# A two-layer hybrid transformer trunk on one core: low parts on VectorE, norms in one operation, attention of the first half as one chain

## The chip, the cores and the metric

One core of one Trainium2 chip runs the whole program. The metric is the device time of one execution in microseconds (us), as the median of several runs. Engines are named as in the profile: PE is TensorE (PEld its weight loads), DVE is VectorE, ACT is ScalarE, POOL is GpSimd, SP issues most loads from memory.

## What is computed

1024 tokens of width 1024 go through two layers, each followed by a squared-ReLU MLP (1024 to 4096 and back). Everything is float32.

```python
# layer 0 (even): h = rms_norm(x); one projection h @ w_in gives
#   A: q (4 heads), one shared k and v, index queries (8 heads x 64), index key, index weights
#   B: q, k, v (4 heads) and a forget gate per head
score = sum_j w_idx[j] * relu(q_idx[j] @ k_idx.T)          # causal
idx = top_k(score, 256)                                     # keys kept for each query
oa = softmax(rms_norm(q) @ rms_norm(k)[idx].T * scale) @ v[idx]
ob = softmax(rms_norm(q) @ rms_norm(k).T * scale + c_q - c_k) @ v   # c: cumulative log forget gate
x += concat(oa, ob) @ w_out;  x += relu(rms_norm(x) @ w1)**2 @ w2
# layer 1 (odd): C multi-head latent attention (low-rank q and k/v, rotary part), D Mamba-2 scan
x += concat(oc, y) @ w_out;   x += relu(rms_norm(x) @ w1)**2 @ w2
```

## The kernel before, in words

**Halves and precision.** The 1024 tokens are worked on in two halves of 512. A float32 product is made of three float32r products: each operand is split into a high part (ACT writes it, `whi` for weights, `xnh` for normed activations) and a low part, the rest (`wlo`, `xnl`), and `mm3` issues high x high, high x low and low x high. `split` writes both parts. `piece` loads weights in pieces of 128x1024 (`wraw`, four buffers), splits them into `whi` and `wlo` (three buffers each), and SP issues the loads.

**Who writes the low parts.** `lo_of` is a list that `piece` rotates: up to the first MLP it is five times POOL and once DVE, from there on DVE alone. In `norm_x` POOL writes `xnl` of every second one of eight chunks, DVE that of the others.

**Projections.** `proj_f` gives results with features on partitions, `proj_t` with tokens on partitions; `proj_t` keeps two blocks of 128 tokens in one PSUM bank when its weights are 256 wide, and calls `done` for each. `qk_pair` projects two heads of queries or keys; `head_norms` takes the sum of squares of each head (ACT) and copies the block to `st` (DVE, L656); `rstd_of` makes reciprocal roots on POOL (L279, L280, a power); `normed_T` scales each 128x128 block by its column of `ss` (DVE, L662, eight for a pair), and later turns the blocks on PE (L667).

**What runs beside what.** A Python generator yields after each small step. `beside(gen, rate)` advances one while a projection is written: every `tick` of the projection advances it by `rate` steps. So `rate` sets how densely PE's order mixes attention into projections. `after(n, fn)` puts a step off by n ticks; `finish` writes the rest of a generator at once. Engines then run their lists in order, each waiting on semaphores.

**Selection** (`topk_masks`): 31 rounds find each query's 256th score bit by bit; in each, ACT counts some blocks with a Sign pass (L825), DVE the others (L860), and DVE updates a candidate (L865 to L869). Its end marks ties and writes masks (L888 to L901), one step for each block. The first half's selection has two blocks, the second half's four (three of them counted by ACT).

**Attention.** `pipe` yields three steps a block: weigh an older block (`po`, L551), turn one (transposes L517, copies to `pt` on ACT, L518), score a new one (L540, then `softmax`: exponential on ACT, reciprocal and scaling on DVE, L527 and L528). `fox_blocks` is B, `dsa_blocks` is A. In the first half B runs at rate 1.5 beside projections of both halves, and is finished; A starts after that, at rate 1.7, beside the output projection of B.

Of the kernel before, what the change touches and what calls it, by code (L numbers as in the profile page):

```python
# [36 lines left out]
def trunk(ctx, tc, a, out):  # L37
# [213 lines left out]

    lo_of = [dve]

    def split(hi, lo, src, scale=None, eng=None):

        if scale is None:
            act.activation(hi, src, AF.Copy)  # L257
            (eng or dve).tensor_sub(lo, src, hi.bitcast(F32))  # L258
        else:
            act.activation(hi, src, AF.Copy, scale=scale)  # L260
            dve.scalar_tensor_tensor(lo, src, scale, hi.bitcast(F32), op0=ALU.mult, op1=ALU.subtract)
# [20 lines left out]
    def piece(parts, kc, n, at=0):  # L282


        subs = []
        per = min(kc, 1024 // n)
        for k0 in range(0, kc, per):
            nk = min(per, kc - k0)
            raw, hi, lo = (wp.tile([P, room], dt, name=nm, tag=nm, bufs=bufs)[:, a0:a0 + nk * n]
                           .rearrange("p (k f) -> p k f", k=nk)  # L290
                           for nm, dt, bufs, room, a0 in (("wraw", F32, 4, 1024, 0), ("whi", F32R, 3, 1088, at),
                                                          ("wlo", F32R, 3, 1088, at)))
            c0 = 0
            for ap in parts:
                w = ap.shape[-1]
                nc.sync.dma_start(raw[:, :, c0:c0 + w], ap[k0 * P:(k0 + nk) * P].rearrange("(k p) f -> p k f", p=P))
                c0 += w
            split(hi, lo, raw, eng=lo_of[0])
            lo_of.append(lo_of.pop(0))
            subs.append((k0, nk, hi, lo))  # L300
        return subs
# [13 lines left out]

    def proj_t(xn, subs, n, done):

# [4 lines left out]
        def part(b, sub):  # L322
# [8 lines left out]
            if k0 + nk == kc and b % per == per - 1:  # L331
                for q in range(per):
                    done(b - per + 1 + q, pss[b // per][:, q * n:(q + 1) * n])
# [111 lines left out]
    def norm_x(half, gain, box):  # L445
        flush(box)
        hi, lo = [], []
        for c in range(DC):
            if c % 2 == 0:
                hi.append(xnp.tile([P, 2, HT], F32R, name="xnh", tag="xnh"))  # L450
                lo.append(xnp.tile([P, 2, HT], F32R, name="xnl", tag="xnl"))
            y = tmp(name="xr")
            dve.scalar_tensor_tensor(y, xc(half, c), gain[:, c:c + 1], box["rb"], op0=ALU.mult, op1=ALU.mult)  # L453
            split(hi[-1][:, c % 2], lo[-1][:, c % 2], y, eng=pool if c % 2 else dve)
        return (lambda k: hi[k // 2][:, k % 2]), (lambda k: lo[k // 2][:, k % 2])
# [193 lines left out]

    def head_norms(ps, b, q, ss, heads, width):  # L650

        for h in range(heads):
            junk = tmp((P, 192), name="junk")
            act.activation(junk[:, :width], ps[:, h * width:(h + 1) * width], AF.Square,
                           accum_out=ss[:, b * heads + h: b * heads + h + 1])
        dve.tensor_copy(q, ps[:, :heads * width])  # L656

    def normed_T(st, heads, h, r, dst, gain):

        for b in range(NB):  # L660
            v = st[:, b, h * P:(h + 1) * P]
            dve.tensor_scalar(v, v, r[:, b * heads + h: b * heads + h + 1], None, op0=ALU.mult)  # L662

# [18 lines left out]
    def qk_pair(xn, w_ap, gain, dst):  # L682

        w = piece([w_ap], 8, 256, MOVING)
        st = g([P, NB, 256], name="st")
        ss = small(NB * 2, "ss")
        proj_t(xn, w, 256, lambda b, ps: head_norms(ps, b, st[:, b], ss, 2, P))
        rstd_of(ss, NB * 2, 128.0, "qk")
        for h in range(2):
            normed_T(st, 2, h, ss, dst[h], gain)  # L690

    def even_proj_index(half, xn):
# [17 lines left out]
        def gates(r):  # L710
# [12 lines left out]
            dve.tensor_sub(lf, lf, z)  # L723
            after(3, sums)

# [84 lines left out]
    def topk_masks(accs, Ls, by_act):  # L810
# [77 lines left out]
        for n, L in enumerate(Ls):  # L888
# [14 lines left out]
    def fox_proj(half, xn, pr):  # L903
# [8 lines left out]
        w = piece([w_in[:, EV_VB + pr * 256: EV_VB + (pr + 1) * 256]], 8, 256, MOVING)  # L912
        proj_t(xn, w, 256, lambda b, ps: act.copy(vb[:, b], ps[:, :256]))
        yield
# [50 lines left out]
    def even_dsa_proj(half, xn):  # L965
# [8 lines left out]
        def done(b, ps):  # L974
            head_norms(ps, b, st[:, b], ss, 1, P)
            act.copy(va[:, b * P:(b + 1) * P], ps[:, P:2 * P])

        proj_t(xn, w, 256, done)
        rstd_of(ss, NB, 128.0, "ka")
        normed_T(st, 1, 0, ss, ka, cols["ka"])  # L980
        yield
# [51 lines left out]
    def odd_low_rank(half, xn):  # L1033
# [30 lines left out]
        for name, r, src in (("cq", rq, [(0, 0), (0, 128), (1, 0)]), ("ckv", rkv, [(1, 128), (2, 0)])):  # L1064
            for c, (n, c0) in enumerate(src):
                for b in range(NB):
                    v = st[n][:, b, c0:c0 + P]
                    dve.tensor_scalar(v, v, r[:, b:b + 1], None, op0=ALU.mult)
                h = new_h("low")
# [11 lines left out]
    def mla_proj(half, pr):  # L1081
# [16 lines left out]
        rstd_of(sq, NB * 2, 192.0, "q")  # L1098
        qT, qrT = [[g([P, 2, HT], F32R, name=k) for _ in range(n)] for k, n in (("qT", 2), ("qrT", 1))]
        for h in range(2):  # L1100
            normed_T(qs, 2, h, sq, (qT[h][:, 0], qT[h][:, 1]), qscale[:, 2:3])

# [21 lines left out]
        def done_kv(b, ps):  # L1124
            for h in range(2):
# [13 lines left out]
        dve.tensor_tensor(krs, kr[:, :, None, :].to_broadcast([P, NB, 2, 64]),  # L1139
                          sk3[:, :, :, None].to_broadcast([P, NB, 2, 64]), op=ALU.mult)  # L1140
        for h in range(2):
            normed_T(ks, 2, h, sk, (kT[h][:, 0], kT[h][:, 1]), cols["kcn"])

# [136 lines left out]
    def ssd_scan(half, gi, hs):  # L1280
# [95 lines left out]
        rstd_of(ss, NB, 256.0, "y")  # L1376
        for b in range(NB):
            dve.tensor_scalar(yg[:, b], yg[:, b], ss[:, b:b + 1], None, op0=ALU.mult)
        yield
# [40 lines left out]

    lo_of[:] = [pool] * 5 + [dve]
    box = row_stats(rows)
# [19 lines left out]

    fox = pipe(chain(fox_blocks(0, 0, hs_a), fox_blocks(0, 1, hs_a)), 2)
    dsa = pipe(dsa_a(), 3)
    beside(fox, 1.5)
    run(fox_proj(0, xn, 1))
# [24 lines left out]

# [122 lines left out]
```

## Time and profile before

| what | value |
|---|---|
| median of 3 runs (lowest to highest) | 2816.67 us (2814.97 to 2818.53) |
| profiled execution: time, span | 2815.35 us, 2813.6 us |
| PE busy | 2723.9 us, 97% |
| PE weight loads | 2324.4 us, 83% |
| DVE, ACT, POOL busy | 1738.2, 1256.1, 743.8 us (62%, 45%, 26%) |
| granted clock of PE, mean | 0.988 |
| chain that ended last | PE 75%, DVE 9%, issue 5%, ACT 5%, POOL 3%, DMA 1% |

The first two slices of forty (some 140 us) show PE at 7 and 8 tenths, all later ones 8 or 9 and more. The granted clock is a share of 2.4 GHz; it has two levels, 1.2 GHz and 2.4 GHz, so that 0.83 over a stretch means that a third of it ran at the lower one. Rows of windows give busy time (and number of instructions) of each engine in a stretch; PE's idle time there is the stretch less PE's busy time. A row of a group of instructions gives busy time and mean duration, and after the second bar the engine's idle time just before them with its releasers.

### The profile page before, as it was taken

What the parts mean: (1) busy time and instruction counts of PE and PEld (TensorE: products, weight loads), DVE (VectorE), ACT (ScalarE), POOL (GpSimd) and SP (SyncE); (2) the same over time, 40 slices, a digit from 0 to 9 for tenths busy, and PEclk for the clock granted to TensorE, in tenths of its full rate; (3) what the DMA queues carried; (4) which work ended last, traced back from release to release, by engine and by line L of the source; (5) the groups of instructions that cost most, each with busy time, mean ns of one, the idle gap of its engine ahead of it and who ended that gap; (6) DMA issues with size and microseconds to landing.
All of it is one profiled execution on the core that took longest, in us unless ns stands there. A gap on an engine that the chain in (4) does not pass through costs nothing.

```text
span 2813.6 us, 39104 instructions
## 1 busy us (share of the span) xinstructions
PE 2723.9 (97%) x14509; PEld 2324.4 (83%) x14509; DVE 1738.2 (62%) x3169; ACT 1256.1 (45%) x2446; POOL 743.8 (26%) x878
## 2 busy tenths in 40 slices
PE   7889999999999999999999999999999999999999
PEld 6888877888788898888888889888887788788887
DVE  5775456877864577764567666775466754634434
ACT  4565335599734355543333334554433323332322
POOL 5335433111100212331344410233134430110110
PEclk8999999999999999999999999999999999999999
DMA  6243433334421426853334552685323463333332
GB/s 175 68 139 121 155 111 90 107 103 143 143 75 61 165 84 165 239 182 105 120 105 153 167 178 80 185 248 168 127 98 120 135 217 98 113 98 98 98 97 68
DMA packets 302964, 365.84 MB, mean 130 GB/s; under 512 B 40611, under 2 KB 258606, under 8 KB 302774
## 3 DMA queue, kind: packets, MB, share of 16 engines
q1 hardware_dynamic: 236550, 223.51, 25.8%
q0 software_dynamic: 66224, 139.84, 15.2%
q8 instruction: 114, 1.87, 0.3%
q14 instruction: 76, 0.62, 0.1%
HBM read 292.16 MB, written 68.70 MB: 128 GB/s over the span
## 4 chain that ended last, share of the span: by engine, by line
PE 75%; DVE 9%; issue 5%; ACT 5%; POOL 3%; DMA 1%; POOLq 0%; DVEq 0%; ACTq 0%
PE pm L273 21%; PE pm L274 21%; PE pm L275 21%; PE po L551 3%; PE pa L540 2%; ACT junk L825 1%; PE pa L517 1%; DVE xr L453 1%; DVE wlo L258 1%; PE py L1342 1%; ACT whi L257 1%; DVE st L662 1%; POOL xnl L258 1%; DVE x L468 1%; POOL rsq L493 1%
## 5 line engine op out<-in xcount | busy, mean ns | idle before, releaser
L257 ACT ACTIVATE whi<-wraw 128x1024 fp32r<-128x1024 f32 (+2 forms) x414 | 434.0, 1049 | 604.0 <-PE pm L274 510.3
L258 DVE TENSOR_TENSOR wlo<-wraw,whi 128x1024 fp32r<-128x1024 f32 (+1 forms) x369 | 462.6, 1254 | 207.4 <-ACT whi L257 187.9
L273 PE MATMUL pm<-xnh,whi 128*128 128x512 f32 (+1 forms) x1360 | 547.4, 404 | 6.0 <-ACT xnh L257 4.9
L274 PE MATMUL pm<-xnl,whi 128*128 128x512 f32 (+1 forms) x1360 | 534.2, 393 | 7.8 <-DVE xnl L258 4.6
L275 PE MATMUL pm<-xnh,wlo 128*128 128x512 f32 (+1 forms) x1360 | 534.1, 393 | 0.0
L273 PE MATMUL pm<-h,whi 128*128 128x512 f32 x1024 | 409.5, 401 | 5.2 <-DVE tk L895 4.5
L274 PE MATMUL pm<-h,whi 128*128 128x512 f32 x1024 | 401.8, 392 | 0.7 <-DVE h L258 0.7
L275 PE MATMUL pm<-h,wlo 128*128 128x512 f32 x1024 | 401.9, 392 | 0.0
L468 DVE TENSOR_TENSOR x<-pm,x 128x512 f32<-128x512 f32 x336 | 231.0, 688 | 270.2 <-PE pm L275 265.3
L493 POOL TENSOR_TENSOR rsq<-relu 128x512 f32<-128x512 f32 x128 | 165.9, 1296 | 824.3 <-ACT relu L491 754.9
L274 PEld LDWEIGHTS pm<-xnl,whi 128*128 128x128 f32 (+1 forms) x1360 | 256.5, 189 | 63.9 <-POOL xnl L258 6.9
L273 PEld LDWEIGHTS pm<-xnh,whi 128*128 128x128 f32 (+1 forms) x1360 | 256.6, 189 | 58.3 <-ACT xnh L257 6.4
L275 PEld LDWEIGHTS pm<-xnh,wlo 128*128 128x128 f32 (+1 forms) x1360 | 256.0, 188 | 55.6 <-issue 0.4
L273 PE MATMUL pm<-whi,xnh 128*128 128x256 f32 x1024 | 298.9, 292 | 0.6 <-DVE st L656 0.6
L275 PE MATMUL pm<-whi,xnl 128*128 128x256 f32 x1024 | 288.4, 282 | 2.0 <-POOL xnl L258 1.1
L274 PE MATMUL pm<-wlo,xnh 128*128 128x256 f32 x1024 | 288.4, 282 | 0.0
L273 PEld LDWEIGHTS pm<-h,whi 128*128 128x128 f32 x1024 | 193.4, 189 | 44.1 <-DVE tk L895 5.2
L275 PEld LDWEIGHTS pm<-h,wlo 128*128 128x128 f32 x1024 | 193.0, 188 | 41.3 <-DVE wlo L258 0.2
L274 PEld LDWEIGHTS pm<-h,whi 128*128 128x128 f32 x1024 | 193.4, 189 | 38.8 <-DVE h L258 1.7
L258 DVE TENSOR_TENSOR h<-rsq,h 128x512 fp32r<-128x512 f32 x128 | 95.2, 743 | 181.7 <-ACT h L257 180.3
L273 PEld LDWEIGHTS pm<-whi,xnh 128*128 128x128 f32 x1024 | 196.2, 192 | 3.8 <-DVE st L656 1.0
L275 PEld LDWEIGHTS pm<-whi,xnl 128*128 128x128 f32 x1024 | 196.3, 192 | 2.6 <-POOL xnl L258 1.5
(651 smaller groups left out, 4508.6 us busy)
## 6 DMA issues: line engine op xcount, KB each, us to landing
wraw<-in_mlp_w_dram SPq DMA_DIRECT2D x256, 512.0 KB
wraw<-in_ev_w_in_dram SPq DMA_DIRECT2D x44, 512.0 KB
wraw<-in_od_w_in_dram SPq DMA_DIRECT2D x40, 512.0 KB
wraw<-in_od_w_out_dram SPq DMA_DIRECT2D x24, 512.0 KB
parked<-x POOLq DMA_DIRECT2D x16, 512.0 KB, 4.0
wraw<-in_ev_w_out_dram SPq DMA_DIRECT2D x16, 512.0 KB
x<-parked POOLq DMA_DIRECT2D x16, 512.0 KB, 7.5
wraw<-in_od_w_in_dram SPq DMA_DIRECT2D x32, 256.0 KB
```

Of the source, the lines that this page charges most:

```text
L257: act.activation(hi, src, AF.Copy)
L258: (eng or dve).tensor_sub(lo, src, hi.bitcast(F32))
L273: pe.matmul(ps, w[0], x[0], start=first, stop=False, skip_group_check=True)
L274: pe.matmul(ps, w[0], x[1], start=False, stop=False, skip_group_check=True)
L275: pe.matmul(ps, w[1], x[0], start=False, stop=last, skip_group_check=True)
L453: dve.scalar_tensor_tensor(y, xc(half, c), gain[:, c:c + 1], box["rb"], op0=ALU.mult, op1=ALU.mult)
L468: dve.tensor_add(x, ps, x)
L493: pool.tensor_mul(sq, r, r)
L517: pe.transpose(ps[:, k * P:(k + 1) * P], p[:, (k0 + k) * P:(k0 + k + 1) * P], ident)
L540: pe.matmul(ps[:, :m], q, kf(k0, m), start=(i == 0), stop=(i == len(mats) - 1))
L551: pe.matmul(po, v(k), pt[:, k, :], start=(k == 0), stop=(k == nk - 1))
L662: dve.tensor_scalar(v, v, r[:, b * heads + h: b * heads + h + 1], None, op0=ALU.mult)
```

## The change

`split` loses its engine argument: all low parts are written by DVE, 45 of weights and 32 of `xnl` that POOL wrote. `proj_t` may hand over a whole bank (`whole`), so that copies to `st`, `vb` and `va` take two blocks at once; `head_norms` copies first and squares then. The scalings by reciprocal roots become one operation that broadcasts `ss` over all heads (`scale_rows`). The first half's attention is one chain, B then A, at rate 1.45. Selection's end yields twice more for each block, its rate in the second half's bit rounds goes from 0.66 to 0.8, and the gate's `sums` is put off by 6 ticks instead of 3.

```diff
-    def split(hi, lo, src, scale=None, eng=None):
+    def split(hi, lo, src, scale=None):
             act.activation(hi, src, AF.Copy)
-            (eng or dve).tensor_sub(lo, src, hi.bitcast(F32))
+            dve.tensor_sub(lo, src, hi.bitcast(F32))
...
-            split(hi, lo, raw, eng=lo_of[0])
-            lo_of.append(lo_of.pop(0))
+            split(hi, lo, raw)
...
             if k0 + nk == kc and b % per == per - 1:
-                for q in range(per):
+                if whole:
+                    done(b - per + 1, pss[b // per])
+                for q in range(0 if whole else per):
                     done(b - per + 1 + q, pss[b // per][:, q * n:(q + 1) * n])
...
-            split(hi[-1][:, c % 2], lo[-1][:, c % 2], y, eng=pool if c % 2 else dve)
+            split(hi[-1][:, c % 2], lo[-1][:, c % 2], y)
...
-    def head_norms(ps, b, q, ss, heads, width):
-        for h in range(heads):
-            junk = tmp((P, 192), name="junk")
-            act.activation(junk[:, :width], ps[:, h * width:(h + 1) * width], AF.Square,
-                           accum_out=ss[:, b * heads + h: b * heads + h + 1])
-        dve.tensor_copy(q, ps[:, :heads * width])
-
-    def normed_T(st, heads, h, r, dst, gain):
-        for b in range(NB):
-            v = st[:, b, h * P:(h + 1) * P]
-            dve.tensor_scalar(v, v, r[:, b * heads + h: b * heads + h + 1], None, op0=ALU.mult)
+    def head_norms(b, ps, st, ss):
+        n = st.shape[-1]
+        heads = n // P
+        v = ps.rearrange("p (b c) -> p b c", b=2)[:, :, :n]
+        dve.tensor_copy(st[:, b:b + 2], v)
+        for q in range(2):
+            for h in range(heads):
+                junk = tmp((P, 192), name="junk")
+                at = (b + q) * heads + h
+                act.activation(junk[:, :P], v[:, q, h * P:(h + 1) * P], AF.Square, accum_out=ss[:, at:at + 1])
+
+    def scale_rows(v, r, groups, n):
+        dve.tensor_tensor(v, v, r[:, :, None].to_broadcast([P, groups, n]), op=ALU.mult)
+
+    def scaled(st, heads, r):
+        scale_rows(st.rearrange("p b (h d) -> p (b h) d", d=P), r, NB * heads, P)
+
+    def normed_T(st, h, dst, gain):
...
-            after(3, sums)
+            after(6, sums)
...
             dve.tensor_scalar(need[:, m], need[:, m], 1.0, 0.5, op0=ALU.add, op1=ALU.mult)
+            yield
             dve.tensor_tensor_scan(rank, eq, eq, 0.0, op0=ALU.add, op1=ALU.max)
             dve.scalar_tensor_tensor(rank, rank, need[:, m], eq, op0=ALU.is_gt, op1=ALU.mult)
+            yield
...
-    lo_of[:] = [pool] * 5 + [dve]
...
-    fox = pipe(chain(fox_blocks(0, 0, hs_a), fox_blocks(0, 1, hs_a)), 2)
-    dsa = pipe(dsa_a(), 3)
-    beside(fox, 1.5)
+    attn = chain(pipe(chain(fox_blocks(0, 0, hs_a), fox_blocks(0, 1, hs_a)), 2), pipe(dsa_a(), 3))
+    beside(attn, 1.45)
     run(fox_proj(0, xn, 1))
...
-    finish(fox)
     unpark(0)
...
-    beside(dsa, 1.7)
     run(add_rows(0, ev_out[512:1024, :], hs_a))
...
-    finish(dsa)
+    finish(attn)
...
-    sides[0][1] = 0.66
+    sides[0][1] = 0.8
```

The same replacement of scalings is made in `even_dsa_proj` (`kst`), `odd_low_rank`, `mla_proj` (`qs`, `ks`) and the scan's `yg`. Over the program DVE's list goes from 3091 to 2940 instructions (77 more low parts, 228 fewer scalings and copies), POOL's from 883 to 806, ACT's from 1960 to 1948, PE's holds the same matmuls.

DVE at the very first `norm_x`, before (`xr` is the scaled chunk):

```order
L453 SCALAR_TENSOR_TENSOR xr_243<-x0_182,cols_ev_125,rb_239 128x512
L453 SCALAR_TENSOR_TENSOR xr_247<-x0_182,cols_ev_125,rb_239 128x512
L453 SCALAR_TENSOR_TENSOR xr_253<-x0_183,cols_ev_125,rb_239 128x512
L258 TENSOR_TENSOR xnl_242<-xr_243,xnh_241 128x512
L453 SCALAR_TENSOR_TENSOR xr_257<-x0_183,cols_ev_125,rb_239 128x512
L258 TENSOR_TENSOR xnl_252<-xr_253,xnh_251 128x512
```

DVE at the same place now:

```order
L256 TENSOR_TENSOR wlo_283<-wraw_281,whi_282 128x608
L453 SCALAR_TENSOR_TENSOR xr_243<-x0_182,cols_ev_125,rb_239 128x512
L453 SCALAR_TENSOR_TENSOR xr_247<-x0_182,cols_ev_125,rb_239 128x512
L453 SCALAR_TENSOR_TENSOR xr_253<-x0_183,cols_ev_125,rb_239 128x512
L256 TENSOR_TENSOR xnl_242<-xr_243,xnh_241 128x512
L256 TENSOR_TENSOR wlo_325<-wraw_323,whi_324 128x1024
L256 TENSOR_TENSOR xnl_242<-xr_247,xnh_241 128x512
L256 TENSOR_TENSOR xnl_252<-xr_253,xnh_251 128x512
```

The weights' low parts and the `xnl` that POOL wrote now stand in DVE's list, after the third `xr`.

DVE where the second pair of heads of B (`st`) is scaled, with selection's rounds (`tkless`, `tkcand`, `tknxt`, `junk`) around it, before:

```order
L865 TENSOR_SCALAR tknxt_1041<-tkcand_971 128x2
L860 TENSOR_SCALAR junk_1039,tkcnt_1036<-isc_616,tkcand_971 128x512
L656 COPY st_791<-pm_830 128x256
L662 TENSOR_SCALAR st_791<-st_791,ss_792 128x128 x8
L867 TENSOR_TENSOR tkless_1043<-tkcnt_1036,tk_922 128x2
```

And now:

```order
L874 TENSOR_SCALAR tknxt_1023<-tkcand_961 128x2
L869 TENSOR_SCALAR junk_1021,tkcnt_1018<-isc_616,tkcand_961 128x512
L664 TENSOR_TENSOR st_782<-st_782,ss_783 128x1024
L876 TENSOR_TENSOR tkless_1025<-tkcnt_1018,tk_912 128x2
L878 SCALAR_TENSOR_TENSOR tkcand_1027<-tkless_1025,tknxt_1023 128x2
L874 TENSOR_SCALAR tknxt_1046<-tkcand_1027 128x2
L869 TENSOR_SCALAR junk_1044,tkcnt_1041<-isc_616,tkcand_1027 128x512
L256 TENSOR_TENSOR wlo_1201<-wraw_1199,whi_1200 128x1024
```

One instruction stands for eight, and a weight's low part follows a round later.

PE at the end of the first half's A (`kva` holds its keys and values, `oa` its output), before:

```order
L275 MATMUL pm_4586<-xnh_2761,wlo_4577 76x512
L540 MATMUL pa_4619<-kva_1962,qa_2269 128x512
L551 MATMUL po_4626<-pt_4559,kva_1962 128x128 x3
L517 MATMUL pa_4633<-ident_96,pa__4429 128x128 x3
L540 MATMUL pa_4640<-kva_1962,qa_2532 128x512
L551 MATMUL po_4647<-pt_4632,kva_1962 128x128 x3
L517 MATMUL pa_4654<-ident_96,pa__4503 128x128 x4
L540 MATMUL pa_4662<-kva_1962,qa_2532 128x512
L551 MATMUL po_4669<-pt_4653,kva_1962 128x128 x4
L517 MATMUL pa_4677<-ident_96,pa__4617 128x128 x4
L273 MATMUL pm_4724<-oa_1203,whi_4719 128x512
```

And now:

```order
L271 MATMUL pm_4557<-xnh_2686,whi_4547 76x512
L272 MATMUL pm_4557<-xnl_2687,whi_4547 76x512
L273 MATMUL pm_4557<-xnh_2686,wlo_4548 76x512
L271 MATMUL pm_4594<-oa_1183,whi_4589 128x512
L272 MATMUL pm_4594<-oa_1183,whi_4589 128x512
```

The last blocks of A stood together with no projection between them; now A's last `po` stands 62 rows ahead of the first use of `oa`.

## Rows read from the trace of the kernel before

**Rows 1.** Windows: stretch and its length, busy us of each engine, PEclk, DMA.
```profile
core 0: us, PE busy (x) PEld busy (x) DVE busy (x) ACT busy (x) POOL busy (x), PEclk, DMA share, GB/s
0.00:50.00 50.00, 35.00 (x141) 25.70 (x142) 31.71 (x60) 23.47 (x45) 27.59 (x69) 0.83 0.65 191
50.00:250.00 200.00, 175.47 (x1306) 164.72 (x1305) 138.47 (x404) 118.56 (x348) 83.51 (x79) 0.94 0.31 96
...
300.00:480.00 180.00, 165.81 (x932) 139.64 (x931) 103.57 (x220) 77.01 (x182) 67.30 (x60) 0.96 0.38 118
480.00:800.00 320.00, 307.96 (x1539) 258.90 (x1538) 254.35 (x505) 238.78 (x431) 48.36 (x72) 0.99 0.37 118
800.00:2814.00 2014.00, 1990.95 (x10175) 1687.19 (x10173) 1188.90 (x1933) 774.32 (x1367) 490.31 (x579) 1.00 0.42 133
```

**Rows 2.** Waits of PE from 50 to 480 us: total, times, longest.
```profile
PE po L551 <- ACT pt L518: 9.8, 9, 2.7
PE pa L667 <- DVE st L662: 8.4, 4, 4.9
PE pa L517 <- DVE fbias L528: 4.5, 2, 3.0
PE pa L728 <- DVE lf L723: 3.6, 1, 3.6
...
PE pa L517 <- DVE pa__3818 L528: 2.1, 1, 2.1
```

**Rows 3.** Timeline around 98 us: start, length, engine, line, operation [idle before].
```profile
97.87 2.34 POOL L258 TENSOR_TENSOR wlo<-wraw,whi 128x1024 fp32r<-128x1024 f32 x1
...
97.94 4.40 DVE L662 TENSOR_SCALAR st<-st,ss 128x128 f32<-128x128 f32 x8 [1.17 <-POOL ss L280]
...
101.12 0.98 PE L667 MATMUL pa<-ident,st 128*128 128x128 f32 x4 [4.89 <-DVE st L662]
```

**Rows 4.** Groups of POOL by line, 0 to 480 us.
```profile
L258 POOL TENSOR_TENSOR wlo<-wraw,whi 128x1024 fp32r<-128x1024 f32 x43 | 104.8, 2446 | 110.0 <-ACT whi L257 105.7 <-issue 4.2
L280 POOL TENSOR_TENSOR ss<-ss,mhalf 128x8 f32<-128x8 f32 x12 | 21.8, 1814 | 1.0
L258 POOL TENSOR_TENSOR xnl<-xr,xnh 128x512 fp32r<-128x512 f32 x12 | 19.3, 1611 | 16.8 <-ACT xnh L257 16.8
```

**Rows 5.** Groups of DVE, 0 to 480 us, then 800 to 2814 us.
```profile
L662 DVE TENSOR_SCALAR st<-st,ss 128x128 f32<-128x128 f32 x96 | 33.7, 427 | 21.2 <-POOL ss L280 21.2
...
L258 DVE TENSOR_TENSOR wlo<-wraw,whi 128x1024 fp32r<-128x1024 f32 x14 | 17.1, 1222 | 5.7 <-ACT whi L257 5.7
...
L258 DVE TENSOR_TENSOR wlo<-wraw,whi 128x1024 fp32r<-128x1024 f32 x306 | 388.3, 1269 | 193.9 <-ACT whi L257 177.1 <-PE pa L1297 10.0 <-PE py L1342 4.4
...
L662 DVE TENSOR_SCALAR qst<-qst,sq 128x128 f32<-128x128 f32 x32 | 6.6, 281 | 5.3 <-POOL sq L280 5.3
...
L1139 DVE TENSOR_TENSOR krs<-krg,sk 128x512 f32<-128x512 f32 x4 | 2.8, 693 | 7.2 <-POOL sk L280 7.2
```

**Rows 6.** Timeline at the start of the program.
```profile
18.10 5.32 POOL L258 TENSOR_TENSOR wlo<-wraw,whi 128x1024 fp32r<-128x1024 f32 x2 [1.26 <-issue]
...
21.15 2.83 DVE L258 TENSOR_TENSOR xnl<-xr,xnh 128x512 fp32r<-128x512 f32 x1
...
24.02 0.71 PE L274 MATMUL pm<-xnl,whi 128*76 128x512 f32 x1 [3.94 <-DVE xnl L258]
```

**Rows 7.** Windows around two stalls, columns as in rows 1.
```profile
96.00:126.00 30.00, 22.15 (x148) 21.19 (x147) 20.67 (x73) 17.15 (x52) 12.59 (x13) 0.83 0.33 106
...
410.00:424.00 14.00, 10.44 (x37) 8.27 (x36) 8.46 (x32) 2.58 (x4) 2.98 (x3) 0.76 0.35 113
```

**Rows 8.** Second half's selection: its window, ACT's passes (min/median/max ns), PE's longest wait.
```profile
556.00:744.00 188.00, 181.79 (x956) 153.76 (x955) 140.46 (x322) 174.30 (x315) 27.06 (x44) 0.99 0.35 113
...
L825 ACT ACTIVATE junk<-isc,tkcand,tk x93: 904/1019/1144, 559.3 to 741.2; 128x640 bf16<-128x640 f32 x31, 128x768 bf16<-128x768 f32 x31, 128x896 bf16<-128x896 f32 x31
...
PE pm L273 <- DVE tk L895: 4.5, 2, 3.4
```

More of the change, by code (lines that the diff above doesn't have):

```diff
@@ L249, in chain @@
             yield from x
-    lo_of = [dve]
-    def split(hi, lo, src, scale=None, eng=None):
+    def split(hi, lo, src, scale=None):
         if scale is None:
             act.activation(hi, src, AF.Copy)
-            (eng or dve).tensor_sub(lo, src, hi.bitcast(F32))
+            dve.tensor_sub(lo, src, hi.bitcast(F32))
         else:
@@ L314, in proj_f, with proj_t @@
                 tick(nk / 4)
-    def proj_t(xn, subs, n, done):
+    def proj_t(xn, subs, n, done, whole=False):
         per = 512 // n
@@ L686, in qk_pair @@
         ss = small(NB * 2, "ss")
-        proj_t(xn, w, 256, lambda b, ps: head_norms(ps, b, st[:, b], ss, 2, P))
+        proj_t(xn, w, 256, lambda b, ps: head_norms(b, ps, st, ss), whole=True)
         rstd_of(ss, NB * 2, 128.0, "qk")
+        scaled(st, 2, ss)
         for h in range(2):
-            normed_T(st, 2, h, ss, dst[h], gain)
+            normed_T(st, h, dst[h], gain)
     def even_proj_index(half, xn):
@@ L912, in fox_proj @@
         w = piece([w_in[:, EV_VB + pr * 256: EV_VB + (pr + 1) * 256]], 8, 256, MOVING)
-        proj_t(xn, w, 256, lambda b, ps: act.copy(vb[:, b], ps[:, :256]))
+        proj_t(xn, w, 256, lambda b, ps: act.copy(vb[:, b:b + 2].rearrange("p b d -> p (b d)"), ps), whole=True)
         yield
@@ L974, in done @@
         def done(b, ps):
-            head_norms(ps, b, st[:, b], ss, 1, P)
-            act.copy(va[:, b * P:(b + 1) * P], ps[:, P:2 * P])
-        proj_t(xn, w, 256, done)
+            head_norms(b, ps, st, ss)
+            act.copy(va[:, b * P:(b + 2) * P].rearrange("p (b d) -> p b d", b=2),
+                     ps.rearrange("p (b c) -> p b c", b=2)[:, :, P:])
+        proj_t(xn, w, 256, done, whole=True)
         rstd_of(ss, NB, 128.0, "ka")
-        normed_T(st, 1, 0, ss, ka, cols["ka"])
+        scaled(st, 1, ss)
+        normed_T(st, 0, ka, cols["ka"])
         yield
@@ L1065, in odd_low_rank @@
             for c, (n, c0) in enumerate(src):
-                for b in range(NB):
-                    v = st[n][:, b, c0:c0 + P]
-                    dve.tensor_scalar(v, v, r[:, b:b + 1], None, op0=ALU.mult)
+                scale_rows(st[n][:, :, c0:c0 + P], r, NB, P)
                 h = new_h("low")
@@ L1099, in mla_proj @@
         qT, qrT = [[g([P, 2, HT], F32R, name=k) for _ in range(n)] for k, n in (("qT", 2), ("qrT", 1))]
+        scaled(qs, 2, sq)
         for h in range(2):
-            normed_T(qs, 2, h, sq, (qT[h][:, 0], qT[h][:, 1]), qscale[:, 2:3])
+            normed_T(qs, h, (qT[h][:, 0], qT[h][:, 1]), qscale[:, 2:3])
         def turned_q():
@@ L1140, in mla_proj @@
                           sk3[:, :, :, None].to_broadcast([P, NB, 2, 64]), op=ALU.mult)
+        scaled(ks, 2, sk)
         for h in range(2):
-            normed_T(ks, 2, h, sk, (kT[h][:, 0], kT[h][:, 1]), cols["kcn"])
+            normed_T(ks, h, (kT[h][:, 0], kT[h][:, 1]), cols["kcn"])
         def turn_k():
@@ L1376, in ssd_scan @@
         rstd_of(ss, NB, 256.0, "y")
-        for b in range(NB):
-            dve.tensor_scalar(yg[:, b], yg[:, b], ss[:, b:b + 1], None, op0=ALU.mult)
+        scale_rows(yg, ss, NB, 256)
         yield
@@ L1483, in trunk @@
     xn = norm_x(0, cols["mlp0"], box)
-    lo_of[:] = [dve]
     idx = chain(scored(1, range(NB)), selected(1, range(NB), 3))
```

## The prediction, made before the changed kernel was run

> **What bounds the kernel now.** I read the windows first. PE is busy for 97% of the span, so nothing but PE's idle time and its clock can give time back, and the windows say where these lie [rows 1]: idle 15.0 us in the first 50 us (50.00 less 35.00), 24.5 in 50 to 250, 14.2 in 300 to 480, 12.0 in 480 to 800, and 23.05 in the 2014 us after that, 1.1%. The granted clock is 0.83, 0.94, 0.96, 0.99 and 1.00 in the same stretches. The change works mostly on the first half of layer 0, so on the 38.7 us (24.5 + 14.2) of 50 to 480.
>
> Next the waits of PE there [rows 2]: 9.8 us for ACT's `pt`, 8.4 for DVE's scaled `st`, 4.5 and 2.1 for DVE's softmax scaling, 3.6 for `lf`. Last the timeline at the longest wait for `st` [rows 3]. Eight scalings begin at 97.94 and take 4.40 us together; POOL's two-input subtract for `wlo` runs from 97.87 to 100.21, across their first half; PE's transposes wait 4.89 us. The groups say the same over the stretch: one scaling costs 427 ns in 0 to 480 us and 281 ns for `qst` after 800 us, where no low parts are on POOL [rows 5]. At the start a DVE `xnl` of 128x512 takes 2.83 us while POOL runs two `wlo` (18.10 to 23.42), and PE waits 3.94 us for it [rows 6]; a DVE `wlo` of twice its size takes 1.222 us on the mean [rows 5]. So DVE is held up while POOL subtracts, and some of PE's waits for DVE are really POOL's doing.
>
> **The change part by part.** Sums go against the profiled execution's own 2815.35 us; the median is 1.3 us above it, and I add that at the end.
>
> *Low parts to DVE.* POOL loses 43 `wlo` of 2446 ns and 12 `xnl` of 1611 ns before 480 us [rows 4] and little after. DVE gains 43 x 1.222 = 52.5 us, and 12 `xnl` at about half of that (0.65, an estimate from the size), 7.8 us. It loses 12 groups of eight scalings (96 x 0.427 = 41) and gets 12 broadcast ones. For these the nearest row is the broadcast `krs`, 693 ns for 128x512 [rows 5], so about 1.39 us for 128x1024: 16.6 us. Net about +36 us on a DVE that is busy 242 of 380 us (138.47 and 103.57, [rows 1]): some 73%, not yet full. What this buys PE goes by place.
>
> (1) Start, 0 to 50 us. The wait of 3.94 us [rows 6] goes, or shrinks by what the `xnl` was stretched (2.83 less about 0.7, 2.1 us); the added low parts ahead of it in DVE's list take a little back. I take -3.0, between 2.1 and 3.9.
>
> (2) Idle time in 50 to 250 and 300 to 480, 38.7 us. The waits for `st` are 8.4; I take 7.4, since one broadcast operation must end before the first transpose may start, where before four scalings were enough (two `krs` lengths, 1.39, against 4 x 0.281 = 1.12: 0.2 to 0.3 us for a pair, some 14 times in the program, 2.5 us at the worst). The waits for the softmax scaling, 4.5 and 2.1, I take whole: such a scaling is one small operation that stood behind a blocked one. The wait for `lf`, 3.6, goes because `sums` is put off by three more ticks, each some microseconds of projection. Of the 9.8 for `pt` I take half, 4.9: the attention becomes sparser (1.45 instead of 1.5 and 1.7 steps a tick), and A's last blocks, which stood in a row with no projection between them, now stand inside projections; but `pt` comes from ACT, which hardly changes. Of the rest, 10.3 us of small gaps, half again, 5.2. Sum -27.7. Bounds: -16.1 if only the waits for DVE and `lf` go (18.6) and the broadcast costs its 2.5; -34.4 if the idle share falls to the 1.1% that the program has after 800 us.
>
> Does the single chain cost anything? A's queries need the selection's masks. Selection has about 46 steps at 1.35 a tick, 34 ticks; B's blocks hold the chain back for about as long, so A finds its masks written, if closely. The chain has 96 steps, 66 ticks at 1.45, and some 70 ticks of projection stand before `finish(attn)`: little is left over to be written in a row. The moved steps are PE, ACT and DVE instructions and no loads of their own; what POOL and SP issue (stash, park, unpark, key reads) passes no longer behind POOL's subtracts, which can only make it earlier. I put this at zero, inside the half of `pt`.
>
> (3) Clock. The lost clock is 200 x 0.06 = 12.0 us and 180 x 0.04 = 7.2 us of full speed [rows 1]; times PE's busy share (0.88 and 0.92) 17.2 us if all came back. It stands around the stalls: 0.83 in the 30 us that begin just before the 4.89 us wait, 0.76 in 14 us at 410, where PE was busy 10.44 [rows 7]. These two alone give 30 x 0.17 x 0.74 + 14 x 0.24 x 0.75 = 6.3. I take -10, somewhat below the middle of 6.3 and 17.2, since gaps of `pt` stay.
>
> (4) 480 to 800. ACT is the busiest beside PE in the second half's selection: 174.3 of 188 us, of it 93 Sign passes of 1.019 us, 94.8 us [rows 8]. The rate 0.8 instead of 0.66 puts the rounds into 188 x 0.66/0.8 = 155 us. ACT's other work there is (174.3 - 94.8)/188 = 0.423 of the time, so it would be asked for 94.8 + 0.423 x 155 = 160.4 us in 155: 5.4 us too much, which PE would wait for at worst. Against it, the two yields a block break up selection's end, behind which PE waited 4.5 us [rows 8]. I take +1, between -4.5 and +5.4.
>
> (5) After 800 us the change only merges scalings (4 to 8 into one) on a DVE busy 1188.90 of 2014 us [rows 1]: 0, within 2 either way.
>
> Sum: -3.0 - 27.7 - 10 + 1 = -39.7, so 2775.7 for a profiled execution, and 2777 as a median. All best bounds together (-3.9, -34.4, -17.2, -4.5, -2) give -62 and 2755; all worst (-2.1, -16.1, -6.3, +5.4, +2) give -17.1 and 2800.
>
> The Trainium skill, page "Perfetto Trace Analysis", section "Optimizing Scalar/DVE Operations", says that if ScalarE and VectorE aren't saturated but cause bubbles elsewhere, breaking up instructions may let work finish sooner. The change does the opposite with the scalings; by that rule the loss is the 2.5 us of (2), while rows 3 show that what made them late was another engine's operation and not their number.
>
> **The rivals.** *Only the blocked operations recover.* The pace of attention is set by ACT's `pt`, and by POOL's reciprocal roots (1.814 us each, [rows 4]) ahead of each scaling, which waits 21.2 us for them in all [rows 5]. Then (2) gives 16.1, (1) 2.0, and the clock nothing, since PE keeps its holes: -18, 2799 as a median. For it: `pt` is the largest single wait [rows 2]. Against it: `pt` itself depends on softmax steps of the blocked DVE.
>
> *Slower: DVE inherits POOL's waiting.* POOL's `wlo` stood 105.7 us waiting for ACT's `whi` [rows 4]; nothing but POOL's own list stood behind it. The same subtracts now stand in DVE's list, ahead of softmax scalings, selection rounds and `st`, and all of these wait in order. 36 more us of work and 106 of waiting on 242 of 380 busy make DVE full (384 of 380). It decides from about two fifths: when 42 of the 106 us reach PE, the gain of 40 is gone; at half, 53, the change costs 13 us and the median is 2830. Against it: in the same stretch DVE already had 14 `wlo`, and they waited 5.7 us, 0.41 each; 43 more at that price are 17.5 us. After 800 us the 306 pieces waited 177.1 us for `whi` on DVE [rows 5], and PE was idle 23.05 us in all [rows 1], so at most 13% of such waiting reached PE. The same page and section of the Trainium skill says that with DVE saturated, offloading to ScalarE or GpSimd may make sense, but that GpSimd and DVE share a read port, so that it might not help. The first half of the sentence speaks for this rival, the second for the forecast; rows 3 and 6 agree with the second (4.40 us for eight scalings under a POOL subtract, 8 x 0.281 = 2.2 by the undisturbed row).
>
> *No change: the stalls move.* Each wait removed only lets PE arrive earlier at the next one, `po` behind `pt`, and the attention chain as a whole keeps its length: 2816. Against it: PE's projections have work of their own between attention steps.
>
> **How the numbers follow.** Forecast 0.66 (2777), blocked operations only 0.20 (2799), DVE inherits the waits 0.07 (2830), stalls move 0.07 (2816). The low end is 2752: the best bounds, 2755, and 3 us for the clock of the first 50 us, 0.83, which is in no term. The high end, 2803, takes in the worst bounds and the first rival, and leaves out the other two and little else, under 2 in 10. About 0.2%, 5.6 us, is what a measurement of this kernel can tell from no change: faster 0.86, same 0.07, slower 0.07.
>
> **What would show it.** Right: no `wlo` or `xnl` among POOL's groups; DVE's `wlo` still about 1.25 us and the broadcast scaling of 128x1024 at 1.2 to 1.5; PE's idle time in 50 to 480 near 11 us instead of 38.7, no wait for `st` above 1 us, the clock in 50 to 250 at 0.97 or more; ACT above 95% in selection's stretch with PE's waits for counts of a few us. Wrong: DVE's `wlo` waiting for `whi` by much over 0.4 us each before 480 us, with PE's waits for softmax scalings grown (the slower rival); idle time gone but the clock as before (term 3); `pt` waits above 10 us (no change); a broadcast scaling well above 1.4 us, the row that (2) leaned on.

## The result, and the profile after

The changed kernel takes 2772.02 us (median of four runs, 2771.28 to 2773.79) against 2816.88 us; the ratio is 0.984 with a 95% interval of 0.9825 to 0.986. The prediction was 2777 in a range of 2752 to 2803. The profiled execution took 2771.28 us with a span of 2769.6, so the profiled executions differ by 44.1 us. The page says where that lies: PE is busy for 2706.2 us instead of 2723.9, 17.7 us less for the same 14509 matmuls, and idle for 63.4 us (2769.6 less 2706.2) instead of 89.7, 26.3 us less. Most of the fall in busy time is the clock, but not all, as the windows of the same work below show.

The windows of the changed kernel, with the columns of [rows 1] (PE, PEld, DVE, ACT, POOL):

```profile
0.00:50.00 50.00, 38.12 (x154) 29.00 (x155) 31.01 (x67) 24.80 (x47) 9.65 (x60) 1.00 0.67 203
50.00:250.00 200.00, 186.19 (x1478) 178.23 (x1477) 146.85 (x387) 130.02 (x378) 38.54 (x61) 0.97 0.36 111
250.00:300.00 50.00, 50.00 (x379) 47.35 (x378) 29.53 (x60) 24.40 (x77) 12.30 (x18) 1.00 0.65 210
300.00:480.00 180.00, 176.06 (x976) 149.71 (x975) 115.02 (x203) 83.12 (x176) 26.42 (x38) 0.99 0.35 107
480.00:800.00 320.00, 305.73 (x1550) 256.25 (x1549) 240.79 (x497) 232.90 (x418) 47.78 (x69) 0.99 0.37 118
```

Idle time in 50 to 250 and 300 to 480 us is 13.8 and 3.9 us, where [rows 1] had 24.5 and 14.2; POOL's busy time there has more than halved (150.8 to 65.0 us), DVE's has grown only from 242 to 262 us. The waits of PE from 50 to 480 us (total, times, longest), which answer to [rows 2]:

```profile
PE po L551 <- ACT pt L518: 5.8, 6, 2.8
...
PE pa L675 <- DVE st L664: 1.9, 2, 1.4
PE pa L675 <- DVE kst L664: 1.4, 1, 1.4
...
PE pa L517 <- DVE fbias L528: 0.9, 1, 0.9
```

Of the 8.4 us for `st` 1.9 are left, of the 4.5 for `fbias` 0.9; `lf` and `pa__3818` are gone. The groups of DVE from 0 to 480 us, which answer to [rows 5]:

```profile
L256 DVE TENSOR_TENSOR wlo<-wraw,whi 128x1024 fp32r<-128x1024 f32 (+1 forms) x65 | 78.6, 1210 | 22.6 <-ACT whi L255 21.0 <-PE pa L415 0.9
...
L453 DVE SCALAR_TENSOR_TENSOR xr<-x,cols_ev,rb 128x512 f32<-128x512 f32 x24 | 17.2, 746 | 0.9 <-ACT rb L443 0.7 <-DMA qst<-qilo 0.2
...
L256 DVE TENSOR_TENSOR xnl<-xr,xnh 128x512 fp32r<-128x512 f32 x24 | 15.8, 685 | 5.6 <-ACT xnh L255 5.6
L664 DVE TENSOR_TENSOR st<-st,ss 128x1024 f32<-128x1024 f32 x12 | 15.0, 1251 | 21.9 <-POOL ss L278 21.9
```

65 low parts waited 21.0 us for ACT, 0.32 each: DVE did not inherit POOL's 105.7 us. The merged scaling takes 1251 ns.

Since the changed kernel runs ahead, a window of equal times holds more work in it. Windows that end at the same projection matmul hold the same work (PE's counts differ by 5 at most). With the columns of [rows 1], which has the first 50 us, before:

```profile
50.00:483.80 433.80, 393.84 (x2676) 355.80 (x2675) 266.56 (x677) 221.71 (x607) 178.61 (x161) 0.96 0.37 116
483.80:816.00 332.20, 320.16 (x1608) 269.49 (x1607) 257.16 (x514) 244.55 (x442) 50.09 (x73) 0.99 0.37 117
816.00:2813.00 1997.00, 1974.95 (x10088) 1673.44 (x10086) 1182.75 (x1921) 766.35 (x1352) 487.54 (x576) 1.00 0.43 134
```

and after:

```profile
0.00:46.10 46.10, 34.22 (x136) 25.76 (x137) 28.16 (x57) 23.16 (x45) 9.65 (x60) 1.00 0.70 215
46.10:444.60 398.50, 381.73 (x2681) 349.58 (x2680) 265.12 (x616) 219.07 (x593) 72.01 (x112) 0.98 0.40 124
444.60:780.00 335.40, 320.15 (x1608) 267.89 (x1607) 258.01 (x516) 245.46 (x445) 51.36 (x73) 0.99 0.37 116
780.00:2769.00 1989.00, 1970.12 (x10088) 1673.85 (x10086) 1176.30 (x1831) 766.62 (x1352) 456.48 (x556) 1.00 0.43 134
```

Stretch by stretch PE is idle for 3.1 and 23.2 us less, 3.2 us more, and 3.2 us less; it is busy for 0.8 and 12.1 us less, the same, and 4.8 us less. The last 4.8 us are not the clock, which is 1.00 in both rows.

To compare all kernels by place in the work I use one more measure. All have 414 weight pieces in the same order, and the table takes the moment at which ACT starts the `whi` of a certain piece, less that moment in the kernel before; the two runs are set equal at the first piece. A column is the change within a stretch, named by the times of the kernel before (pieces 0, 6, 30, 60, 102, then the end). Each row is one profiled execution, so differences of 2 us mean little.

```
kernel                       median    0-50  50-263  263-484  484-816  816-end
changed                      2772.0    -4.1   -17.8    -16.3     +2.1     -8.1
e1  low parts alone          2768.7    -1.7   -20.1    -11.9     +0.2    -11.5
e2  all but the low parts    2799.6    -0.1    -6.3    -13.5     +4.5     +1.1
e3  + POOL two inputs        2806.0    -2.7    +8.5     -9.0     +2.0     -7.9
e4  + POOL one input         2790.3    -6.4    -0.8    -13.4     +3.5     -4.9
e11 + POOL writes only       2777.6    -6.6   -11.5    -14.9     +3.6     -8.3
e5  split scalings           2772.9    -3.8   -16.7    -17.3     +4.1     -8.2
e7  two chains               2772.4    -3.9   -19.6    -15.6     +4.0     -5.5
e6  0.66, no steps           2769.1    -3.7   -19.1    -16.4     -0.1     -5.5
e9  0.66, steps              2773.7    -3.9   -18.1    -16.4     +3.8     -7.2
e10 0.8, no steps            2784.2    -3.9   -19.1    -16.2    +16.5     -8.4
e8  e5 and e6 together       2768.8    -3.5   -15.9    -16.1     -0.1     -8.3
e12 xnl alone                2808.2    +1.7    +0.1     -0.4     +0.5     -9.5
```

### The profile page after: what moved, and what is told of

Its sections match the earlier page's. It is cut to its first block, busy times and chain, and to the rows that moved or that the text cites. A ratio compares the mean times of both kernels' runs of the same rounds, so it can differ in the third digit from the quotient of the medians.

```text
span 2769.6 us, 38862 instructions
## 1 busy us (share of the span) xinstructions
PE 2706.2 (98%) x14509; PEld 2317.1 (84%) x14509; DVE 1727.6 (62%) x3018; ACT 1254.3 (45%) x2434; POOL 589.5 (21%) x801
## 4 chain that ended last, share of the span: by engine, by line
PE 80%; issue 6%; DVE 5%; ACT 5%; POOL 2%; DMA 1%; SPq 0%; POOLq 0%; DVEq 0%; ACTq 0%
PE pm L271 23%; PE pm L272 23%; PE pm L273 23%; PE pa L540 3%; PE po L551 3%; ACT junk L834 2%; PE pa L517 1%; PE py L1355 1%; POOL rsq L493 1%; DVE wlo L256 1%; ACT whi L255 1%; DVE junk L869 1%; ACT junk L660 1%; PE pa L675 1%; DVE isc L811 0%
## 5 line engine op out<-in xcount | busy, mean ns | idle before, releaser
L256 DVE TENSOR_TENSOR wlo<-wraw,whi 128x1024 fp32r<-128x1024 f32 (+2 forms) x414 | 514.8, 1244 | 222.4 <-ACT whi L255 202.7
L272 PEld LDWEIGHTS pm<-wlo,xnh 128*128 128x128 f32 x1024 | 194.0, 190 | 2.9 <-issue 1.7
```

The costliest lines, as they stand in the source:

```text
L256: dve.tensor_sub(lo, src, hi.bitcast(F32))
L272: pe.matmul(ps, w[0], x[1], start=False, stop=False, skip_group_check=True)
```

## The experiments

**The low parts alone, and everything but them.** Theory: POOL's subtracts hold DVE up, and that is most of the gain. Rival: it is the chain and the merged scalings. The first run edits the kernel before:

```diff
-    lo_of[:] = [pool] * 5 + [dve]
+    lo_of[:] = [dve]
-            split(hi[-1][:, c % 2], lo[-1][:, c % 2], y, eng=pool if c % 2 else dve)
+            split(hi[-1][:, c % 2], lo[-1][:, c % 2], y, eng=dve)
```

> The kernel before, with one edit: all low parts on VectorE, none on GpSimd. Theory (GpSimd's two-input subtracts hold VectorE up, and that is most of the gain): 2788 to 2795 us, the single scaling near 281 ns instead of 427, the wait of PE for st below 3 us instead of 8.4, the clock in the first 50 us above 0.9. Rival (the gain is that of the single attention chain and the merged scalings): 2805 or more. Rival (VectorE inherits GpSimd's waiting): slower than 2817, with VectorE's wlo waiting much over 0.4 us each.

The second gives the changed kernel those lines back as they were before.

> The changed kernel, with GpSimd's low parts given back to it as before (five pieces of six up to the first MLP, every second xnl). Theory: 2793 to 2802 us, that is, only some 15 to 23 of the 45 us are left, and the broadcast scaling of 128x1024 takes much over its 1.25 us where a subtract of GpSimd lies beside it. Rival (chain and merged scalings make the gain): 2782 or less.

The low parts alone give 2768.7 us, ratio 0.983 (0.9815 to 0.984): all of the gain, and more than the theory had asked for. The rest alone gives 2799.6, ratio 0.994 (0.992 to 0.995), as expected; in it one of the twelve merged scalings met a subtract of POOL, and took 3.35 us. The gains, 47.8 and 16.9 us, don't add: both together give 44.9. The waits of PE in 50 to 480 us, low parts alone:

```profile
PE pa L517 <- DVE tkless L867: 3.3, 1, 3.3
PE pa L667 <- DVE st L662: 2.8, 2, 1.8
...
PE po L551 <- ACT pt L518: 2.5, 3, 1.1
...
PE pa L728 <- DVE lf L723: 0.8, 2, 0.6
```

and its scalings of `st`, still eight at a time:

```profile
L662 DVE TENSOR_SCALAR st<-st,ss 128x128 f32<-128x128 f32 x96 | 20.7, 290 | 16.8 <-POOL ss L280 16.8
```

290 ns instead of 427. The wait for `pt` fell from 9.8 to 2.5 us with the old two chains, and that for `lf` from 3.6 to 0.8 with `sums` put off by 3 ticks as before. So these were waits of the same cause, one step further down, and the edits aimed at them could only remove what the low parts remove as well.

**What it is in POOL's work.** The changed kernel gets an extra operation of POOL for as many pieces as POOL served before, 45 (five of six, though it leaves out the piece just ahead of the one that DVE had). Only the line with `pool` differs between the three runs; the cut shows all three forms together, with comments added.

```diff
             split(hi, lo, raw)
+            also.append(also.pop(0))    # five of six pieces, up to the first MLP
+            if also[0]:
+                pool.tensor_sub(raw, raw, hi.bitcast(F32))                    # two inputs
+                pool.tensor_scalar(raw, raw, 1.0, None, op0=ALU.mult)         # or one input
+                for _ in range(3): pool.memset(raw, 0.0)                      # or none
```

> The changed kernel (VectorE writes all low parts), and GpSimd subtracts once more, in place into the raw weights whose result nobody reads, for the same five pieces of six up to the first MLP. No result of it is waited for except that the raw buffer comes free later. Theory (it is GpSimd's two-input operation beside VectorE that costs): VectorE's operations stretch again and 10 to 20 us are lost, 2782 to 2792. Rival (before, the low part itself came late, since GpSimd took 2.4 us for it): within 4 us of the changed kernel, 2772 to 2776.

> As the kernel with the extra GpSimd subtract, but the extra operation has one input (times 1.0, in place), for the same pieces and with the same buffers held. Theory (it is the two inputs): within 4 us of the changed kernel. Rival (any work of GpSimd, or the raw buffers held longer, costs): as much as the extra subtract.

> As the kernels with an extra operation of GpSimd on the raw weights, for the same pieces, but the extra work is three memsets in place (about as long together as the one-input operation, 2.8 us, and reading nothing). Theory (the 18 us of the one-input operation are mostly GpSimd's list: its selects and reciprocal roots stand behind the extra work, and raw buffers come free later): 2784 to 2792, with the broadcast scaling of st back at 1.25 us. Rival (what costs is GpSimd reading beside VectorE): 2771 to 2777.

They give 2806.0, 2790.3 and 2777.6 us: 34, 18 and 6 us more than the changed kernel. With two inputs the waits of PE in 50 to 480 us are back near those of before ([rows 2]):

```profile
PE po L556 <- ACT pt L523: 10.2, 5, 3.1
PE pa L680 <- DVE st L669: 8.2, 3, 5.7
PE pa L742 <- DVE lf L737: 3.9, 1, 3.9
```

The instructions that scale the merged `st` (min/median/max ns), with two inputs:

```profile
L669 DVE TENSOR_TENSOR st<-st,ss x12: 1224/3374/3423, 76.0 to 396.3; 128x1024 f32<-128x1024 f32 x12
```

with one input:

```profile
L669 DVE TENSOR_TENSOR st<-st,ss x12: 1224/2064/2070, 73.2 to 383.4; 128x1024 f32<-128x1024 f32 x12
```

and with none:

```profile
L670 DVE TENSOR_TENSOR st<-st,ss x12: 1224/1225/1291, 73.6 to 370.6; 128x1024 f32<-128x1024 f32 x12
```

The same operation takes 1.22 us where it is alone, 2.06 beside a POOL operation that reads one tile, 3.37 beside one that reads two; seven of the twelve lie beside one, the other five take 1.22 to 1.30 us. Not every operation of DVE is held up so: the copies from PSUM to `st`, some of which also lie beside such an operation, take 0.67 to 0.69 us in all three runs and in the changed kernel. The three kinds of extra work are about equally long, 2.44, 2.81 and 2.87 us (3 x 0.957) a piece by their groups. Two inputs:

```profile
L301 POOL TENSOR_TENSOR wraw<-wraw,whi 128x1024 f32<-128x1024 f32 (+1 forms) x45 | 109.5, 2435 | 116.5 <-DVE wlo L258 68.4 <-ACT qa L684 13.4 <-DVE tkless L881 9.6
```

One input:

```profile
L301 POOL TENSOR_SCALAR wraw<-wraw 128x1024 f32<-128x1024 f32 (+1 forms) x45 | 126.2, 2805 | 102.0 <-DVE wlo L258 49.4 <-issue 17.1 <-ACT qa L684 11.2
```

Writes only:

```profile
L302 POOL MEMSET wraw<- 128x1024 f32 (+1 forms) x135 | 127.4, 957 | 97.6 <-DVE wlo L258 76.9 <-ACT qa L685 9.4 <-ACT xnh L257 4.5
```

So with two inputs the theory held, but the price was 34 us and not 10 to 20. And neither POOL's time, nor its list, nor the raw buffers held longer can be the main cost; those are much the same in all three, and the third prices them at 6 us. My expectation for one input fell (within 4 us; it cost 18), and so did the repair of it (that the 18 were POOL's list and late buffers, 2784 to 2792). What holds DVE up is POOL reading beside it. Whether POOL's low parts also came late by themselves in the kernel before was not measured apart; before 480 us PE waited 2.5 us for POOL's `xnl` there and never for its `wlo`.

**The merged scalings.** The changed kernel with one scaling for each block again, in place of `scaled` and for `yg`:

```diff
-        scale_rows(st.rearrange("p b (h d) -> p (b h) d", d=P), r, NB * heads, P)
+        for h in range(heads):
+            for b in range(NB):
+                v = st[:, b, h * P:(h + 1) * P]
+                dve.tensor_scalar(v, v, r[:, b * heads + h: b * heads + h + 1], None, op0=ALU.mult)
```

> The changed kernel with its broadcast scalings of st, kst, qs, ks and yg taken apart again into one operation for each 128x128 block (128x256 for yg); all else stays. Theory (with no subtract of GpSimd beside it, the merged operation only makes the first transpose wait longer): 2 to 5 us faster than the changed kernel, 2767 to 2770, most of it after 800 us, with the wait of PE for yg at 3.7 instead of 5.5. Rival (fewer operations relieve VectorE): 2772 or slower.

2772.9 against 2772.0 us: no difference that can be told, and nothing gained after 816 us. The theory fell.

**The single chain.** The changed kernel with B at 1.5 and A at 1.7, each finished where it was before:

> The changed kernel with the first half's attention as before: B at 1.5, finished, then A at 1.7, finished. Theory (the single chain still pays, since A's bare last blocks go, but less than was forecast, because all else of the change without the low parts gave only 17 us): 2774 to 2779, with PE's waits for pt before 480 us grown. Rival (with the low parts on VectorE the waits at the end of A vanish anyway): within 2 us of 2772.

2772.4 us: the rival holds. The single chain moves time within the stretch (at the piece of 384 us it is 16.7 us ahead of before, where the two chains are 28.6 ahead) and both have made 38 to 39 us by 484.

**Selection.** Its two edits, undone together and one at a time:

```diff
-    sides[0][1] = 0.8
+    sides[0][1] = 0.66
...
-            yield
             dve.tensor_tensor_scan(rank, eq, eq, 0.0, op0=ALU.add, op1=ALU.max)
             dve.scalar_tensor_tensor(rank, rank, need[:, m], eq, op0=ALU.is_gt, op1=ALU.mult)
-            yield
```

> The changed kernel with selection as before: rate 0.66 in the second half's rounds, and no extra steps at its end. Theory (the denser rounds cost a little, since ScalarE was 93% busy there, and give nothing): 1 to 3 us faster, 2769 to 2771, the stretch from 484 to 816 us of before some 2 us shorter. Rival (the edit pays): 2774 or slower.

> The changed kernel with the rate of the second half's selection rounds at 0.66 again; the smaller steps at selection's end stay. Theory (the rate is what costs 3 to 4 us there, the steps save part of the 4.5 us that PE waits behind selection's end): 2765 to 2769, and the stretch from 484 to 816 us of before 0 to 4 us shorter than before. Rival (the steps cost, the rate does not): 2771 or more.

> The changed kernel with the rate of 0.8, and without the smaller steps at selection's end. Theory (the rate costs): 2772 to 2777, the stretch from 484 to 816 us 2 to 5 us longer than before, with the new waits of PE for softmax scalings (fbias 5.1) still there. Rival (the steps cost): 2769 or less.

Both undone: 2769.1, as expected, and the stretch from 484 to 816 us is at -0.1 instead of +2.1. Steps alone: 2773.7 (+3.8 in the stretch), against what I expected. The rate alone: 2784.2, ratio to before 0.989 (0.9875 to 0.990), and +16.5, far more than expected. So the edits are not separate: the steps take back most of what the rate costs, and at the old rate they cost something themselves (4.6 us, in ratios whose intervals overlap). The windows of 700 to 740 us of the rate alone, columns as in [rows 1]:

```profile
700.00:720.00 20.00, 14.85 (x73) 11.42 (x71) 20.00 (x34) 8.63 (x13) 0.29 (x1) 0.93 0.16 53
720.00:740.00 20.00, 16.79 (x70) 14.06 (x71) 11.46 (x13) 6.71 (x12) 7.56 (x9) 0.73 0.61 192
```

and of the changed kernel:

```profile
700.00:720.00 20.00, 20.00 (x112) 17.26 (x111) 16.88 (x27) 10.96 (x17) 4.23 (x5) 1.00 0.39 127
720.00:740.00 20.00, 20.00 (x90) 16.55 (x89) 18.96 (x25) 7.73 (x10) 7.17 (x8) 1.00 0.90 281
```

At the denser rate the end of selection, unbroken, fills DVE for 20 of 20 us; PE is idle for 8.4 us (40 less 14.85 and 16.79) and pays once more with a granted clock of 0.73. Broken into steps it leaves DVE 3 us free, and PE doesn't stop. At the old rate the waits of PE are, from 480 to 800 us, with both undone:

```profile
PE pm L271 <- DVE tk L904: 4.5, 2, 3.4
PE pa L517 <- DVE fbias L528: 2.8, 4, 1.3
```

and with the steps alone:

```profile
PE pm L271 <- DVE x L468: 6.8, 2, 3.5
```

The 4.5 us for the last mask become 6.8 for rows of `x`: I suppose that it depends on the tick into which the finer steps fall, but no run tests that.

**Selection and the merged scalings undone together.** The low parts on DVE and the single chain stay, with split scalings and selection as before:

> Both undone, split scalings and selection as before, in the changed kernel; the low parts on VectorE and the single chain stay. Theory (the two costs add): 2765 to 2768, faster than both kernels and than the one with the low parts alone (2768.7). Rival (they overlap): no faster than the better of the two alone.

2768.8 us, no faster than selection as before alone (2769.1): the rival holds, since split scalings give nothing. This kernel, that one and the low parts alone are all at 2769. They lie 3 us, 0.1%, under the changed kernel, with intervals that overlap; I don't call any of them faster than it.

**The late gain.** 8.1 us came after 816 us, where I had forecast none. The kernel before, with only `xnl` moved:

```diff
-            split(hi[-1][:, c % 2], lo[-1][:, c % 2], y, eng=pool if c % 2 else dve)
+            split(hi[-1][:, c % 2], lo[-1][:, c % 2], y, eng=dve)
```

> The kernel before, with only the low parts of normed activations (xnl) moved from GpSimd to VectorE; the weights' low parts stay on GpSimd. Theory (the 8 to 11 us gained after 816 us come from xnl, the only low parts that GpSimd still wrote there): 2803 to 2809, of it 8 to 11 us after 816 us. Rival (the late gain has another source): 2812 or more.

2808.2 us, ratio 0.997 (0.996 to 0.998), and -9.5 us after 816 us, while the stretches ahead change by 2 at most. Between 800 and 2814 us POOL of the kernel before still had this group:

```profile
L258 POOL TENSOR_TENSOR xnl<-xr,xnh 128x512 fp32r<-128x512 f32 x20 | 30.0, 1501 | 40.2 <-ACT xnh L257 37.4 <-PE pm L275 2.8
```

The gain lies where `norm_x` stands. Up to the same projection matmul it is 0.6, 2.2, 0.7, 3.7 and 2.6 us at the five of them, about 980, 1210, 1655, 1910 and 2435 us. At two of these PE of the kernel before waited for `xnl`, 2.4 us in all, 1.8 of them for POOL's own `xnl`; two of the waits, 1905 to 1941 us:

```profile
1910.63 0.50 PE L274 MATMUL pm<-xnl,whi 128*128 128x512 f32 x1 [0.46 <-POOL xnl L258]
...
1918.47 0.50 PE L274 MATMUL pm<-xnl,whi 128*128 128x512 f32 x1 [0.41 <-DVE xnl L258]
```

None of these is left in the run with `xnl` moved, and PE's waits for DVE's rows of `x` after 800 us fall from 3.2 to 0.9 us. The rest of the 9.5 us, of it 3.6 us less busy time of PE, is not put down to single waits. In the first half the same edit is worth nothing, since POOL's `wlo` hold DVE there as before: PE then waits 4.6 us for a DVE `xnl`.

## Why the prediction was right, and where it was not

*The diagnosis held.* DVE was held up while POOL subtracts: moving the low parts gives the whole gain, and giving POOL a useless subtract of the same size takes 34 of the 45 us back. The forecast, 2777, is 5 us above the result; the sum was -39.7 against -44.1. That it came so near is in part luck: (2) gave 4.5 us less than forecast, (5) 8.1 more.

*(1) Start*, -3.0 forecast: PE's idle time over the same work falls by 3.1 us (15.0 to 11.9), and the wait for DVE's `xnl` is gone. The clock gave little there, though the row has 0.83 before and 1.00 after: in the kernel before, matmuls of 128x512 take 0.63 us up to 29 us and 0.39 from 30 us on. In the changed kernel they do the same some 5 us earlier, so the lower level was there too:

```profile
20.83 0.63 PE L272 MATMUL pm<-xnl,whi 128*76 128x512 f32 x1
...
25.29 0.39 PE L272 MATMUL pm<-xnl,whi 128*76 128x512 f32 x1
```

In the other kernels tried the row has 0.86 to 0.93, and their start in the table lies between -6.6 and +1.7: this term isn't steady to 2 us.

*(2) Idle time in 50 to 480 us*, -27.7 forecast: from 38.7 to 17.7 by equal times, and 23.2 us less over the same work, inside the bounds (-16.1 to -34.4). The waits named went nearly as forecast (`st` 6.5 of 7.4, `fbias` 3.6 of 4.5, `lf` and `pa__3818` whole, `pt` 4.0 of 4.9, 20 of 22.5 us); of the many small gaps, where I took half, 5.2, only some 2 to 3 came back. So two of my signs did not come: idle time near 11 us, and no wait for `st` above 1 us (the longest is 1.4). Two steps were right for a wrong reason. I credited `lf` to the six ticks and half of `pt` to the single chain; with the low parts alone `lf` falls to 0.8 and `pt` to 2.5. The price of the single chain, put at nothing, is nothing.

The merged scaling was estimated at 1.39 us from `krs` and takes 1.25. Its price of up to 2.5 us isn't seen: split scalings give 2772.9. The Trainium skill, page "Perfetto Trace Analysis", section "Optimizing Scalar/DVE Operations", says that breaking up operations may let work finish sooner where an engine isn't saturated; for these scalings no run shows it, and for selection's end the runs show it at the rate of 0.8, though DVE was full there (2784.2 without steps, 2772.0 with them), and not at 0.66.

*(3) Clock*, -10 forecast: in 50 to 480 us the rows give 200 x 0.03 x 0.93 + 180 x 0.03 x 0.98 = 10.9, as forecast. PE's busy time fell by more over the program, 17.7: 12.1 of it between 50 and 484 us, 0.8 before and 4.8 after 816, where the clock was 1.00 before and after. Those 4.8 us belong to (5). The 3 us that the low end of the range took for the clock of the first 50 us did not come.

*(4) 480 to 800*, +1 forecast: +2.1 by the pieces, +3.2 by the windows of the same work, but as the remainder of two larger effects that I had not seen as such. ACT did come above the 95% expected (77.85 of 80 us, 97%):

```profile
560.00:640.00 80.00, 73.34 (x374) 60.88 (x375) 60.38 (x136) 77.85 (x143) 10.40 (x18) 0.96 0.39 126
...
600.00:620.00 20.00, 14.07 (x72) 11.46 (x72) 15.27 (x33) 19.98 (x38) 1.43 (x3) 0.83 0.23 79
```

Where ACT is full, 600 to 620 us, PE waits 4.2 us for a softmax scaling (`fbias`) and the granted clock of these 20 us is 0.83; at the old rate the longest such wait is 1.3 us. My worst case of 5.4 us counted ACT's surplus alone and not what stands behind it, DVE at selection's end, where the rate without the steps costs 16.5.

*(5) After 800 us*, 0 within 2 forecast: -8.1, of which 3.2 us are idle time and 4.8 busy time of PE. This step failed. I wrote that POOL's low parts after 480 us were "little", though `norm_x` gave it every second chunk to the end: 20 subtracts, 30 us of POOL. Moving `xnl` alone gives -9.5 there. Some of it is the mechanism of (2), which I didn't apply there (PE waited for DVE's `x` and `xnl`), and some is POOL's own `xnl` coming late; no run separates the two.

*The rivals.* DVE inherited little: its wait for `whi` was 0.32 us a piece, below the 0.41 that [rows 5] gave; PE waits for `wlo` nowhere before 480 us. The first rival, only blocked operations recover, fell too, since `pt` was such an operation's follower, and so did the third, no change. The same section of the Trainium skill says that GpSimd and VectorE share a read port, so that offloading from one to the other might not help; the traces agree for operations that read (1.22 us becomes 2.06 or 3.37), and show no such stretch beside GpSimd operations that only write (1.22).

## What to carry to other kernels

Before costing an engine's operation at its own duration, look at what runs beside it: the same kind of scaling was 281 ns in one stretch and 427 in another, and that row told more than the share of busy time, which was lower for POOL than for any engine. When several edits aim at waits that have one cause, don't add up what each removes: here 47.8 and 16.9 us made 44.9. And look for a mechanism wherever its operation stands, by the group over the whole span, not only where it hurts most.

## What was not expected of the hardware

A VectorE operation of 1.22 us took 2.06 us beside a GpSimd operation with one input of 128x1024, 3.37 beside one with two, and 1.22 beside memsets of about the same total length. I had expected no cost from one input. And an idle gap of PE can cost twice: 8.4 us of waiting between 700 and 740 us went with a granted clock of 0.93 and 0.73 there, where the kernel without the gap had 1.00.
